# Shared weight pieces for two token streams at stage ends, four more modulation chunks on VectorE, and two holds in VectorE's queue

## Chip, cores and metric

One core of one Trainium2 chip runs the whole kernel in one launch. The metric is the device time of one execution in microseconds (us). The kernel before was run three times: median 2183.82 us, from 2181.91 to 2188.89.

## What is computed

The reference is two stacks of layers. The first has two layers on 256 tokens of 1024 channels (RMS norm, one wide projection, four kinds of mixing, output projection, residual) and a final norm. The second has two layers on two **streams**, the 256 latent tokens `x` (the first stack's output) and 256 context tokens `ctx`. Both go through the same weights, each with its own modulation:

```
for l in range(2):
    mod_l = silu(c) @ ada_w[l] + ada_b[l];  mod_c = silu(c_ctx) @ ada_w[l] + ada_b[l]   # 9 chunks of 1024 each
    xl = post_norm(xl, 0.5 * g1 * swiglu(modulate(xl, sh1, sc1), ffn1_w_in[l], ffn1_w_out[l]))   # "f1"; xc likewise
    yc, yl = even_mixer(...) if l == 0 else odd_mixer(...)       # gated linear attention + latent attention / windows
    xl = post_norm(xl, g2 * yl)
    xl = post_norm(xl, 0.5 * g3 * swiglu(modulate(xl, sh3, sc3), ffn2_w_in[l], ffn2_w_out[l]))   # "f2"
    # xc the same in layer 0; in layer 1 the context ends with f1 and its keys and values
```

`post_norm` adds the branch to `sqrt(2)` times the row and normalises it to mean 0 and variance 1; `modulate` scales and shifts by two chunks. The feed-forward width is 22 blocks of 128.

## The kernel before, in words

**Products in three parts.** Each fp32 product is made of three matmuls (`mm3`, L432 to 436): high by high, high by low, low by high. A weight **piece** of 128x1024 comes by a DMA of 512 KB on SyncE's queue (`wraw`, L394); ScalarE makes its high part `wh` (L353, called from `wload`), VectorE its low part `wl` by a subtraction (L428). There are four buffers each of the raw piece, `wh` and `wl`.

**Order.** The program is traced in Python order, and a planner then orders each engine's queue by its own estimate of when operands are ready, earlier traced first. Once built, the order in a queue is fixed, and an instruction that waits holds up all behind it. `issue_after(i)` makes what is traced under it stand behind `i` in the queue of `i`'s engine; it makes no other wait. `self.hold` is a list by which the next calls of `wload` put their ScalarE cast behind a given instruction.

**Modulation.** The 18 chunks (2 layers x 9) are vector by matrix products, made in one of two ways. `ada` (L600) does it on TensorE: 8 pieces per chunk, small matmuls (L620), for which it is a generator that `fill` advances between other steps. `ada_v` (L645) does it on VectorE: 8 steps per chunk, each one piece by DMA and two `scalar_tensor_tensor` with accumulation (L660), one per stream, advanced by `fillv`. Lists `V1`, `V2`, `V3` say which chunks VectorE makes during f1 of layer 0, f2 of layer 0 and f1 of layer 1: 5, 3 and 3. The other seven are TensorE's: (0,0), (0,1), (0,2) in the first stack, and (0,6), (0,7), (0,8), (1,1) later. `VR` has the steps per input tile and per output step.

**Feed-forward for two streams** (`ffn_two`, L866). Blocks of hidden columns go in groups of 8, 8 and 6. In the first group the first `F0` input tiles are done for ctx alone and then for x alone (so that x's norm has work beside it, 256 columns per matmul), the rest for both at once (512 columns). The last group's output products go stream by stream, ctx first: half n=0 of the 1024 output columns, then n=1, each with its own load of its 3 pieces (2 blocks each), so 12 loads; then the norm of that stream (`tail`, L769, interleaved with the last products, or `layernorm`, L581), and its modulation for the next stage (`xt_mod`, L542: 16 transposes on TensorE, L527, and for each of 8 blocks scale and shift, L558 or ScalarE, a cast to XTH on ScalarE and a subtraction to XTL, L560), put off by a few piece loads (`defer`). ctx's norm and modulation thus have x's products of both halves beside them.

**Mixer output** (`mixer_out`, L918) is the same in layer 0 with 4 pieces per half and stream: 16 loads. **Values of the odd mixer** (`odd_values`, L1761): per stream and half 4 pieces, 16 loads; x's modulation is flushed when its deferral runs out.

**Stage ends.** I number the five places where a norm and a modulation stand between stages: end 1 is f1 of layer 0 to the even mixer, end 2 the mixer output to f2, end 3 f2 to f1 of layer 1, end 4 f1 to the odd mixer, end 5 the odd mixer's output to f2 of layer 1 (x alone, `ffn_one`, L838).

Of the kernel before, what the change touches and what calls it, by code (L numbers as in the profile page):

```python
# [243 lines left out]
class Kern:  # L244
    def __init__(self, ctx, tc, A, out, stage=None):
# [29 lines left out]
        self.later, self.hold = [], []  # L275
# [129 lines left out]
    def wload(self, src, off, w, share=None):  # L405
        nc = self.nc
        if self.later:
            self.later[0][0] -= 1
            if self.later[0][0] < 0:
                with self.tc.issue_after(self.lastmm.ins):  # L410
                    self.later.pop(0)[1]()
        raw = self.wraw(src, off, w)
        h = self.wp.tile([P, 1024], F32R, tag="wh", name=f"wh{self.nm}", bufs=WB[1])
        hold = None
        if self.hold:
            hold = self.hold.pop(0)
# [12 lines left out]
        self.lastp = i  # L429
        return h, lo  # L430
# [287 lines left out]
    def ffn_in_steps(self, wi, ft, hid, ts, hs, pool, tag, share=None):  # L718

        nc = self.nc  # L720
        N = ts.stop - ts.start
        if N == 256:
            b = self.bank(tag)
            pgu = (b[:, :256], b[:, 256:])
        else:
            pgu = (self.bank(tag), self.bank(tag))
        for j in range(2):
            h, lo = self.wload(wi, (2 * ft + j) * 1024, 1024, share)
# [8 lines left out]
        self.split(hid[:, 0, hs], hid[:, 1, hs], pgu[1])  # L737
        yield
# [30 lines left out]
    def tail(self, rows, mul, gb, first, tag, done=None):  # L769
# [3 lines left out]
        for m, z in enumerate(rows):  # L773
# [3 lines left out]
            for i, (a, b) in enumerate(parts):  # L777
                o = self.bank(tag)
                mul(o[:, a:b], m, a, b)
                t = o[:, a:b]  # L780
# [15 lines left out]
            if m:  # L796
                h = slice(512, D)
                nc.vector.tensor_scalar(z[:, :512], z[:, :512], mv[:, 0:1], y, op0=OP.subtract, op1=OP.mult)
            self.act(z[:, h], z[:, h], AF.Identity, scale=y, bias=nb)
            if done:  # L800
                done(m)

# [63 lines left out]
    def ffn_two(self, name, l, pool, order, after, fills=(0, 0), vr=(0, 0), early={}):  # L866
# [8 lines left out]
        for f0 in range(0, NFT, G):  # L875
# [5 lines left out]
            if f0 == 0:  # L881
                for w in order:
# [3 lines left out]
                    for ft in range(0 if w == 0 else len(early), F0):  # L886
                        self.ffn_in(wi, ft, hid[ft], ts, ts, pool, "B", GX)
# [15 lines left out]
            else:  # L903
# [3 lines left out]
                for w in order:  # L907
                    for _ in self.ffn_out(wo, 0, f0, f1, hid, tiles(w), "A"):
                        pass
                    if TL[2 * (2 * l + int(name[1]) - 1) + w]:  # L910
                        self.ffn_tail(wo, f0, hid, tiles(w))
                    else:
                        for _ in self.ffn_out(wo, 1, f0, f1, hid, tiles(w), "A"):
                            pass
                        self.layernorm((self.X, self.C)[w])
                    self.defer(lambda w=w: after(w), DF[0] if w else DF[1])

    def mixer_out(self, src, l, who, pool):  # L918
        self.pnext = PN[4]
        gb = self.gate_rows(l, 1, who, pool)  # L920
        rows = (self.X, self.C)[who]
        outs = self.xs(src, 0, 512, 256 * who, 2)
        for m in range(2):
            self.accum(rows[m], 0, outs[m], gb, True)
        if TL[6 + who]:
            self.xs_tail(src, 4096, 256 * who, rows, gb)
        else:
            outs = self.xs(src, 4096, 512, 256 * who, 2, rows=ROWS)
            for m in range(2):
                self.accum(rows[m], 1, outs[m], gb, True)  # L930
            self.layernorm(rows)
# [40 lines left out]
    def layer1(self, l, b1):  # L972
# [13 lines left out]
        if l == 0:  # L986
# [774 lines left out]
    def odd_values(self, e, order):  # L1761
        V = [self.tl(e, [P, D], f"nv{m}") for m in range(4)]
        for w in order:
            for n in range(2):
                outs = self.xs(self.A["na"], 16 * 1024 + n * 4096, 512, 256 * w, 2)
                for m in range(2):
                    self.copy_any(V[2 * w + m][:, n * 512:(n + 1) * 512], outs[m])
# [50 lines left out]
    def run(self):  # L1818
# [47 lines left out]
        with tc.tile_pool(name="xd", bufs=1) as xc:  # L1866
# [3 lines left out]
            with tc.tile_pool(name="mo", bufs=1) as g:  # L1870
                self.gbn, self.accp = 1, g
                self.mixer_out(A["evo"], 0, 1, g)
                if stage > 5:
                    self.defer(lambda: self.xt_mod(0, 6, 1), DF[2])
                self.mixer_out(A["evo"], 0, 0, g)
                if stage > 5:
                    self.defer(lambda: self.xt_mod(0, 6, 0), DF[3])
# [110 lines left out]
```

## Time and profile before

| | |
|---|---|
| median of three runs | 2183.82 us |
| the profiled execution, its own time | 2177.1 us |
| its span, first to last instruction | 2175.3 us |
| around the span | 1.8 us |
| TensorE busy | 2097.1 us, 96% |
| VectorE, ScalarE busy | 1512.4 us, 70%; 868.0 us, 40% |
| mean granted TensorE clock | 0.986 |
| read from HBM | 332.94 MB |

The engines are named PE (TensorE), PEld (its weight loads), DVE (VectorE), ACT (ScalarE), POOL (GpSimd). PEclk is the granted TensorE clock: 1.00 is 2.4 GHz, 0.50 is 1.2 GHz. An engine's busy time says how much of a stretch it had an instruction running; in a stretch where TensorE is busy throughout, only less work on it shortens the time, and where it is idle, what it waited for does.

### The profile page before, as it was taken

What the parts mean: (1) busy time and instruction counts of PE and PEld (TensorE: products, weight loads), DVE (VectorE), ACT (ScalarE), POOL (GpSimd) and SP (SyncE); (2) the same over time, 40 slices, a digit from 0 to 9 for tenths busy, and PEclk for the clock granted to TensorE, in tenths of its full rate; (3) what the DMA queues carried; (4) which work ended last, traced back from release to release, by engine and by line L of the source; (5) the groups of instructions that cost most, each with busy time, mean ns of one, the idle gap of its engine ahead of it and who ended that gap; (6) DMA issues with size and microseconds to landing.
All of it is one profiled execution on the core that took longest, in us unless ns stands there. A gap on an engine that the chain in (4) does not pass through costs nothing.

```text
span 2175.3 us, 31944 instructions
## 1 busy us (share of the span) xinstructions
PE 2097.1 (96%) x12484; PEld 1769.3 (81%) x12484; DVE 1512.4 (70%) x2746; ACT 868.0 (40%) x1493; POOL 40.0 (2%) x78
## 2 busy tenths in 40 slices
PE   7999999999999899998999999899999989998998
PEld 5898798888877787887888888888888868887997
DVE  6977866667778775868466656846665676776666
ACT  5555545222223534544322223532222255654443
POOL 1000000000000000000000000000000010000000
PEclk9999999999999999999999999999999999998999
DMA  8545547656665312347444545544453364424663
GB/s 283 194 149 177 158 145 245 205 176 202 201 203 178 100 57 67 119 147 240 134 126 146 164 118 154 174 126 136 140 170 113 110 188 145 105 86 138 188 182 123
DMA packets 94903, 337.84 MB, mean 155 GB/s; under 512 B 11357, under 2 KB 12477, under 8 KB 94753
## 3 DMA queue, kind: packets, MB, share of 16 engines
q1 hardware_dynamic: 87552, 314.78, 46.8%
q0 software_dynamic: 5856, 17.39, 2.7%
q10 hardware_dynamic: 1344, 3.64, 0.5%
q8 instruction: 98, 1.61, 0.3%
q14 instruction: 53, 0.43, 0.1%
HBM read 332.94 MB, written 3.20 MB: 155 GB/s over the span
## 4 chain that ended last, share of the span: by engine, by line
PE 87%; DVE 7%; DMA 2%; ACT 2%; issue 2%; SPq 0%; ACTq 0%; DVEq 0%
PE pB L434 13%; PE pB L436 12%; PE pB L435 12%; PE pA L436 10%; PE pA L435 10%; PE pA L434 10%; PE pB L1483 2%; PE pF L434 2%; PE pF L436 2%; PE pF L435 2%; DVE wl L428 1%; PE pP L434 1%; PE pP L435 1%; PE pP L436 1%; DMA wr<-in_ada_dram 1%
## 5 line engine op out<-in xcount | busy, mean ns | idle before, releaser
L353 ACT ACTIVATE wh<-wr 128x1024 fp32r<-128x1024 f32 (+4 forms) x460 | 480.2, 1047 | 1022.5 <-issue 490.8
L428 DVE TENSOR_TENSOR wl<-wr,wh 128x1024 fp32r<-128x1024 f32 (+4 forms) x460 | 553.1, 1204 | 335.6 <-ACT wh L353 332.2
L434 PE MATMUL pB<-XTH,wh 128*128 128x512 f32 (+1 forms) x1552 | 539.3, 348 | 6.8 <-DVE hid L441 4.0
L436 PE MATMUL pB<-XTH,wl 128*128 128x512 f32 (+1 forms) x1552 | 535.3, 345 | 5.6 <-DVE wl L428 5.6
L435 PE MATMUL pB<-XTL,wh 128*128 128x512 f32 (+1 forms) x1552 | 535.6, 345 | 0.4 <-DVE XTL L560 0.4
L434 PEld LDWEIGHTS pB<-XTH,wh 128*128 128x128 f32 x1552 | 294.5, 190 | 48.5 <-DVE hid L441 4.4
L436 PEld LDWEIGHTS pB<-XTH,wl 128*128 128x128 f32 x1552 | 294.5, 190 | 43.9 <-DVE wl L428 5.8
L435 PEld LDWEIGHTS pB<-XTL,wh 128*128 128x128 f32 x1552 | 294.4, 190 | 38.2 <-DVE XTL L560 0.6
L435 PE MATMUL pA<-wl,hid 128*128 128x512 f32 (+1 forms) x624 | 239.5, 384 | 2.6 <-DVE wl L428 2.6
L436 PE MATMUL pA<-wh,hid 128*128 128x512 f32 (+1 forms) x624 | 239.5, 384 | 0.0
L434 PE MATMUL pA<-wh,hid 128*128 128x512 f32 (+1 forms) x624 | 238.0, 383 | 0.0
L660 DVE SCALAR_TENSOR_TENSOR vj<-wr,cb 128x1024 f32<-128x1024 f32 x176 | 214.9, 1221 | 11.7 <-DMA wr<-in_adav_dram 8.3
L736 DVE TENSOR_TENSOR pB<-ft,pB 128x512 f32<-128x512 f32 (+1 forms) x97 | 55.7, 574 | 136.2 <-PE pB L436 134.9
L435 PEld LDWEIGHTS pA<-wl,hid 128*128 128x128 f32 x624 | 117.2, 188 | 27.3 <-DVE wl L428 3.8
L434 PEld LDWEIGHTS pA<-wh,hid 128*128 128x128 f32 x624 | 117.1, 188 | 24.9 <-issue 0.6
L436 PEld LDWEIGHTS pA<-wh,hid 128*128 128x128 f32 x624 | 117.2, 188 | 22.8
L435 PE MATMUL pA<-wl,XTH 128*128 128x512 f32 (+4 forms) x336 | 125.0, 373 | 5.6 <-DVE wl L428 5.5
L434 PE MATMUL pA<-wh,XTH 128*128 128x512 f32 (+4 forms) x336 | 125.6, 376 | 0.4 <-ACT wh L353 0.4
L436 PE MATMUL pA<-wh,XTL 128*128 128x512 f32 (+4 forms) x336 | 125.5, 374 | 0.0
L575 DVE TENSOR_TENSOR pA<-pA,gb 128x512 f32<-128x512 f32 x84 | 58.0, 695 | 31.9 <-PE pA L436 31.7
L435 PEld LDWEIGHTS pA<-wl,XTH 128*128 128x128 f32 x336 | 64.7, 193 | 17.3 <-DVE wl L428 6.9
L434 PEld LDWEIGHTS pA<-wh,XTH 128*128 128x128 f32 x336 | 64.9, 193 | 12.3 <-ACT wh L353 0.7
(456 smaller groups left out, 2949.3 us busy)
## 6 DMA issues: line engine op xcount, KB each, us to landing
wr<-in_f1i_dram SPq DMA_DIRECT2D x108, 512.0 KB, 4.4
wr<-in_f2i_dram SPq DMA_DIRECT2D x94, 512.0 KB, 4.0
wr<-in_adav_dram SPq DMA_DIRECT2D x88, 512.0 KB, 3.9
wr<-in_ada_dram SPq DMA_DIRECT2D x56, 512.0 KB, 4.3
wr<-in_f1o_dram SPq DMA_DIRECT2D x56, 512.0 KB, 3.7
wr<-in_f2o_dram SPq DMA_DIRECT2D x50, 512.0 KB, 3.6
wr<-in_w_dram SPq DMA_DIRECT2D x40, 512.0 KB, 4.3
wr<-in_na_dram SPq DMA_DIRECT2D x32, 512.0 KB, 3.6
```

The source lines that it names most:

```text
L353: self.lasta = self.nc.scalar.activation(out, in_, func, **kw)
L428: i = eng.tensor_sub(lo[:, :w], raw[:, :w], h[:, :w].bitcast(F32))
L434: nc.tensor.matmul(out, lh, rh, start=start, stop=False)
L435: nc.tensor.matmul(out, lh, rl, start=False, stop=False)
L436: self.lastmm = nc.tensor.matmul(out, ll, rh, start=False, stop=stop)
L575: nc.vector.tensor_mul(p, p, gb[:, cs])
L660: nc.vector.scalar_tensor_tensor(junk, raw, 0.5 * f, cb[:, w], op0=OP.mult, op1=OP.mult, accum_out=gc[:, w, k:k + 1])
L736: nc.vector.tensor_mul(pgu[1], t, pgu[1])
L1483: nc.tensor.matmul(p[:, c0 + j * P:c0 + (j + 1) * P], K[r, j * 256 + tk * P:j * 256 + (tk + 1) * P], Q[r, j * 256 + tq * P:j * 256 + (tq + ...
```

## The change

VectorE gets 15 chunks in place of 11: V1 has 6, V2 has 4, V3 has 5; TensorE keeps the three of the first stack. A second list of holds, `holdl`, does for VectorE's subtraction of a piece what `hold` does for the cast: it is set to one entry after the last scaling of each first-stack layer's norm, and to four entries after the last tail's normalisation of end 5. `both_out` makes both streams' output products of a last group: one set of pieces for half n=0 of all four row tiles, one for n=1; after the first row tile of x's n=1 the modulation of ctx is put in (behind the last matmul so far). `mixer_out` and `ffn_two` use it. `ffn_two` keeps the pieces of ctx's last `F0` tile and does that tile first for x. `odd_values` goes ctx n=0, ctx n=1, x n=1 with the same pieces, x n=0.

```diff
-V1 = ((0, 3), (0, 4), (0, 5), (1, 0), (1, 2))
-V2 = ((1, 3), (1, 4), (1, 5))
-V3 = ((1, 6), (1, 7), (1, 8))
-VR = ((2.0, 0.5), (1.25, 0.25), (1.25, 0.25))
+V1 = ((0, 3), (0, 4), (0, 5), (0, 6), (0, 7), (0, 8))
+V2 = ((1, 0), (1, 1), (1, 2), (1, 3))
+V3 = ((1, 4), (1, 5), (1, 6), (1, 7), (1, 8))
+VR = ((2.4, 0.5), (1.75, 0.25), (2.2, 0.25))
...
-        i = eng.tensor_sub(lo[:, :w], raw[:, :w], h[:, :w].bitcast(F32))
+        hold = self.holdl.pop(0) if self.holdl else None
+        with self.tc.issue_after(hold.ins) if hold else ExitStack():
+            i = eng.tensor_sub(lo[:, :w], raw[:, :w], h[:, :w].bitcast(F32))
...
+    def both_out(self, pieces, mul, streams, first, ends, tag, after):
+        ws = pieces(0)
+        alls = streams[0][1] + streams[1][1]
+        self.row_products(ws, lambda o, i, a, b: mul(ws, o, alls[i], a, b), alls, 0, first, tag)
+        w1 = pieces(1)
+        for i, (rows, tiles) in enumerate(streams):
+            def hook():
+                if i == 1:
+                    with self.tc.issue_after(self.lastmm.ins):
+                        after(0)
...
+            if ends[i]:
+                self.tail(rows, m1, tiles[0][1], first, tag, hook=hook)
+            else:
+                self.row_products(w1, m1, tiles, 1, first, tag, hook)
+                self.layernorm(rows)
+        after(1)
...
+                    fs = list(range(0 if w == 0 else len(early), F0))
+                    if keep:
+                        fs = fs[-1:] + fs[:-1]
+                    for ft in fs:
+                        self.ffn_in(wi, ft, hid[ft], ts, ts, pool, "B", GX, keep if ft == F0 - 1 else None)
...
+        self.holdl = [scaled]
         self.fill(FB1[0][l])
         self.xt_scaled(xn, self.cols[:, C_NW + 8 * l:C_NW + 8 * l + 8], 0)
...
-                self.gbn, self.accp = 1, g
-                self.mixer_out(A["evo"], 0, 1, g)
...
+                self.gbn, self.accp = 2, g
+                self.mixer_out(A["evo"], 0, g, lambda i: self.defer(lambda: self.xt_mod(0, 6, 0), DF[3]) if i
+                               else self.xt_mod(0, 6, 1))
...
                     self.xt_mod(1, 6, 0)
+                    self.holdl = [self.lastn] * 4
```

## Rows read from the trace of the kernel before

**Rows 1.** Page, part 1: busy us, share of the span, instructions.

```profile
PE 2097.1 (96%) x12484; PEld 1769.3 (81%) x12484; DVE 1512.4 (70%) x2746; ACT 868.0 (40%) x1493; POOL 40.0 (2%) x78
```

**Rows 2.** Busy time by stretch, stage ends 1 to 5: length, busy, PEclk, DMA, GB/s.

```profile
684.00:725.00 41.00, 33.72 (x199) 28.55 (x200) 35.75 (x92) 14.02 (x25) 3.31 (x7) 0.92 0.57 185
1011.00:1028.00 17.00, 11.54 (x84) 10.13 (x84) 13.58 (x27) 10.49 (x21) 0.00 (x0) 1.00 0.88 324
1377.50:1390.00 12.50, 6.94 (x39) 6.73 (x37) 11.49 (x30) 4.04 (x7) 0.54 (x1) 0.73 0.50 158
1758.00:1789.00 31.00, 22.02 (x89) 17.43 (x88) 21.37 (x51) 14.83 (x25) 5.54 (x9) 0.83 0.76 220
1961.00:1994.00 33.00, 22.37 (x144) 20.97 (x144) 20.21 (x42) 14.64 (x26) 0.56 (x1) 0.79 0.48 144
```

**Rows 3.** Busy time by stretch, L620 alone: length, PE, PEld, PEclk, DMA.

```profile
350.00:700.00 350.00, 11.18 (x320) 8.26 (x320) 1.00 0.63 202
700.00:1000.00 300.00, 8.76 (x192) 5.40 (x192) 0.95 0.33 105
```

**Rows 4.** Page, part 5, groups of L428 and L660: busy, mean ns, idle before.

```profile
L428 DVE TENSOR_TENSOR wl<-wr,wh 128x1024 fp32r<-128x1024 f32 (+4 forms) x460 | 553.1, 1204 | 335.6 <-ACT wh L353 332.2
L660 DVE SCALAR_TENSOR_TENSOR vj<-wr,cb 128x1024 f32<-128x1024 f32 x176 | 214.9, 1221 | 11.7 <-DMA wr<-in_adav_dram 8.3
```

**Rows 5.** Busy time by stretch, f1 of layer 0: last input tiles, last output products.

```profile
595.00:667.00 72.00, 72.00 (x365) 57.33 (x363) 52.20 (x75) 19.48 (x26) 0.00 (x0) 1.00 0.60 192
668.00:690.00 22.00, 20.71 (x93) 16.34 (x89) 21.95 (x36) 7.27 (x9) 2.23 (x4) 1.00 0.49 152
```

**Rows 6.** Busy time by stretch, even mixer, around its second fall of the clock.

```profile
867.20:877.50 10.30, 10.04 (x50) 7.72 (x48) 6.93 (x11) 1.07 (x2) 1.14 (x2) 0.50 0.23 67
```

**Rows 7.** Timeline, DVE, start of the kernel: start, us, instruction, idle before.

```profile
8.70 0.21 DVE L373 TENSOR_SCALAR nwt<-nwt 128x1 f32<-128x1 f32 x1
11.19 1.20 DVE L428 TENSOR_TENSOR wl<-wr,wh 128x1000 fp32r<-128x1000 f32 x1 [2.28 <-ACT wh L353]
...
13.30 0.75 DVE L984 TENSOR_SCALAR xn<-X,nwy 128x1024 f32<-128x1024 f32 x1
```

**Rows 8.** Timeline, DVE, the second layer's norm.

```profile
170.03 1.22 DVE L428 TENSOR_TENSOR wl<-wr,wh 128x1024 fp32r<-128x1024 f32 x1
```

**Rows 9.** Groups of instructions, PE, 172.3 to 178.2 us: busy, mean ns, idle before.

```profile
L436 PE MATMUL pG<-XTH,wl 128*128 128x256 f32 x16 | 4.6, 285 | 0.0
```

**Rows 10.** Timeline, DVE, end 1: first and last of the context's chain.

```profile
686.39 1.29 DVE L575 TENSOR_TENSOR pA<-pA,gb 128x512 f32<-128x512 f32 x2
...
710.31 0.76 DVE L560 TENSOR_TENSOR XTL<-pF,XTH 128x256 fp32r<-128x256 f32 x2
```

**Rows 11.** Timeline, DVE, end 3: the context's chain and the piece behind it.

```profile
1360.56 0.69 DVE L575 TENSOR_TENSOR pA<-pA,gb 128x512 f32<-128x512 f32 x1
...
1380.80 0.42 DVE L560 TENSOR_TENSOR XTL<-pF,XTH 128x256 fp32r<-128x256 f32 x1
...
1382.75 1.17 DVE L428 TENSOR_TENSOR wl<-wr,wh 128x1024 fp32r<-128x1024 f32 x1
```

**Rows 12.** Timeline, PE, two matmuls of 512 columns one after the other.

```profile
1359.04 0.39 PE L435 MATMUL pA<-wl,hid 128*128 128x512 f32 x1
1359.27 0.39 PE L436 MATMUL pA<-wh,hid 128*128 128x512 f32 x1
```

**Rows 13.** Waits, ACT, first from 1003 to 1019 us, then from 1765 to 1780 us: total, times, longest.

```profile
ACT wh L353 <- DMA wr<-in_f2i_dram: 8.5, 4, 4.8
...
ACT wh L353 <- DMA wr<-in_na_dram: 9.2, 3, 6.7
```

**Rows 14.** Timeline, DVE, end 5: first and last subtraction ahead of the norm.

```profile
1962.45 1.22 DVE L428 TENSOR_TENSOR wl<-wr,wh 128x1024 fp32r<-128x1024 f32 x1
...
1965.38 1.20 DVE L428 TENSOR_TENSOR wl<-wr,wh 128x1024 fp32r<-128x1024 f32 x1
...
1968.78 0.54 DVE L798 TENSOR_SCALAR X<-X,lnmv,nwy 128x512 f32<-128x512 f32 x1
```

More of the change, by code (lines that the diff above doesn't have):

```diff
@@ L274, in __init__ @@
         self.ptn = 3
-        self.later, self.hold = [], []
+        self.later, self.hold, self.holdl = [], [], []
         self.vfrac = 0.0
@@ L727, in ffn_in_steps @@
         for j in range(2):
-            h, lo = self.wload(wi, (2 * ft + j) * 1024, 1024, share)
+            if ws and len(ws) == 2:
+                h, lo = ws[j]
+            else:
+                h, lo = self.wload(wi, (2 * ft + j) * 1024, 1024, share)
+                if ws is not None:
+                    new.append((h, lo))
             self.ws(pgu[j], h, lo, ts)
@@ L767, in ffn_out, with tail @@
             self.accum(z, n, o, gb, f0 == 0)
-    def tail(self, rows, mul, gb, first, tag, done=None):
+    def tail(self, rows, mul, gb, first, tag, done=None, hook=None):
         nc = self.nc
@@ L779, in tail @@
                 mul(o[:, a:b], m, a, b)
+                if hook and m == 0:
+                    hook()
                 t = o[:, a:b]
@@ L801, in tail, with row_products, m1 @@
                 done(m)
+    def row_products(self, ws, mul, tiles, n, first, tag, hook=None):
+        for i, (z, gb, _) in enumerate(tiles):
+            o = self.bank(tag)
+            mul(o, i, 0, 512)
+            if hook and i == 0:
+                hook()
+            self.accum(z, n, o, gb, first)
+    def both_out(self, pieces, mul, streams, first, ends, tag, after):
[8 more added lines that the diff above has]
+                        after(0)
+            def m1(o, m, a, b):
+                mul(w1, o, tiles[m], a, b)
+            if ends[i]:
+                self.tail(rows, m1, tiles[0][1], first, tag, hook=hook)
+            else:
+                self.row_products(w1, m1, tiles, 1, first, tag, hook)
+                self.layernorm(rows)
+        after(1)
     def ffn_tail(self, wo, f0, hid, tiles, done=None):
@@ L906, in ffn_two @@
                 self.fillv(1000)
[L907 to L916, printed above, removed]
@@ L918, in mixer_out @@
-    def mixer_out(self, src, l, who, pool):
-        self.pnext = PN[4]
[L920 to L931, printed above, removed]
+                us = range(f0, NFT, 2)
@@ new lines, in mul @@
+                def mul(ws, o, t, a, b):
+                    for u, w in zip(us, ws):
+                        for j in range(2):
+                            hh, s = hid[u + j - f0], slice(t[2], t[2] + P)
+                            js = slice(j * 512 + a, j * 512 + b)
+                            self.mm3(o, hh[:, 0, s], hh[:, 1, s], w[0][:, js], w[1][:, js], u + j == f0, u + j == NFT - 1)
+                k = 2 * (2 * l + int(name[1]) - 1)
+                self.both_out(lambda n: [self.wload(wo, (n * NFT + u) * 512, 1024) for u in us], mul,
+                              [((self.X, self.C)[w], tiles(w)) for w in order], False, [TL[k + w] for w in order], "A",
+                              lambda i: self.defer(lambda: after(order[1]), DF[1]) if i else after(order[0]))
@@ new lines, in mixer_out, with mul @@
+    def mixer_out(self, src, l, pool, after):
+        self.pnext = PN[4]
+        streams = []
+        for w in (1, 0):
+            gb = self.gate_rows(l, 1, w, pool)
+            rows = (self.X, self.C)[w]
+            streams.append((rows, [(rows[m], gb, 256 * w + m * P) for m in range(2)]))
+        def mul(ws, o, t, a, b):
+            s = slice(t[2], t[2] + P)
+            for k in range(8):
+                w, js = ws[k // 2], slice(k % 2 * 512 + a, k % 2 * 512 + b)
+                self.mm3(o, self.XTH[:, k, s], self.XTL[:, k, s], w[0][:, js], w[1][:, js], k == 0, k == 7)
+        self.both_out(lambda n: [self.wload(src, n * 4096 + 1024 * u, 1024) for u in range(4)], mul, streams, True,
+                      (TL[7], TL[6]), "A", after)
@@ L1762, in odd_values, with put @@
         V = [self.tl(e, [P, D], f"nv{m}") for m in range(4)]
-        for w in order:
-            for n in range(2):
-                outs = self.xs(self.A["na"], 16 * 1024 + n * 4096, 512, 256 * w, 2)
-                for m in range(2):
-                    self.copy_any(V[2 * w + m][:, n * 512:(n + 1) * 512], outs[m])
+        src, o = self.A["na"], 16 * 1024
+        a, b = order
+        def put(w, n, outs):
+            for m in range(2):
+                self.copy_any(V[2 * w + m][:, n * 512:(n + 1) * 512], outs[m])
+        put(a, 0, self.xs(src, o, 512, 256 * a, 2))
+        ws = []
+        for w in (a, b):
+            outs = [self.pA(), self.pA()]
+            for u in range(4):
+                if w == a:
+                    ws.append(self.wload(src, o + 4096 + u * 1024, 1024))
+                elif u == 0:
+                    self.flush()
+                for m in range(2):
+                    s = slice(256 * w + m * P, 256 * w + (m + 1) * P)
+                    for j in range(2):
+                        js = slice(j * 512, (j + 1) * 512)
+                        self.mm3(outs[m], self.XTH[:, 2 * u + j, s], self.XTL[:, 2 * u + j, s], ws[u][0][:, js], ws[u][1][:, js],
+                                 u + j == 0, u == 3 and j == 1)
+            put(w, 1, outs)
+        put(b, 0, self.xs(src, o, 512, 256 * b, 2))
         return V
```

17 lines of the change are left out of this document (8 added, 9 removed).

## The prediction

> **What bounds it now.** I read the page's busy shares first: TensorE is busy for 96% of the span, VectorE for 70% [rows 1]. So two things shorten the time: work taken off TensorE where it never idles, and the waits that hold it up. Next I looked where TensorE idles, by busy time in stretches, and found most of it at the stage ends [rows 2]: length less busy is 7.3, 5.5, 5.6, 9.0 and 10.6 us at ends 1 to 5, 38 of the 78 us that are idle in all. The reader should see PEclk there too. It is 0.92, 1.00, 0.73, 0.83 and 0.79, and as the clock has two levels, the share at 1.2 GHz is twice what is missing: 6.6, 0, 6.8, 10.5 and 13.9 us, in which up to half is lost wherever TensorE works. Then the queue of VectorE: it is busy 21.95 of 22 us before end 1 [rows 5] and 11.5 of 12.5 at end 3 [rows 2]. A piece's subtraction for the next stage stood at 1382.75 behind the rest of the context's and latents' norms [rows 11], and TensorE stood for it. A stage end is a VectorE problem.
>
> **Part 1: four chunks from TensorE to VectorE.** In f1 of layer 0 TensorE spends 11.2 us on L620 [rows 3] at full business (72.00 of 72.00 us in a sample of it [rows 5]). That goes, and with it some 2 us of transposes and one wait on those loads; call it 13. In the even mixer L620 holds 8.8 us [rows 3]. There the work is a chain of short products with gaps that the chunks fill, so the gain lies between 0 and 8.8; I take 4. VectorE gains 4 chunks of 16 operations at 1221 ns [rows 4]: 78 us. It loses subtractions of shared pieces: 8 in the mixer output, 18 in three feed-forward ends, 6 by the kept tile, 4 in the values, 36 at 1204 ns [rows 4], 43 us; ScalarE loses as many casts, SyncE's queue as many of 512 KB. Does VectorE have room? Input tiles of f1 are the densest: 52.2 of 72 us [rows 5], a little over six tiles; 0.4 steps more per tile are 2.4 steps of 2.44 us, giving 58 of 72, 81%. TensorE had no idle time at 73%, and 1.3 us in 22 at full VectorE [rows 5]. The cost thus lies between 0 and that share of 15 such tiles' 180 us, 11 us; 81% is nearer the first, so 0. By the rates in VR the first feed-forward makes 2.4x15 + 0.5x16 = 44 of 48 steps on its way, before it was 38 of 40, so two more steps plus the last tile's 0.4, some 6 us of VectorE, fall into end 1. Two transfers swap queues with nothing: both kinds are 512 KB on SyncE's.
>
> **Part 2: pieces for both streams.** TensorE's products are the same. At a feed-forward end six subtractions go, 7.2 us, at the mixer output eight, 9.6 us, out of stretches where VectorE is full. In exchange the context's chain (last sum, norm, 16 transposes, modulation) loses cover. Before, all of x's products stood beside it; now only x's n=1: two row tiles of 18 matmuls at 0.23 us [rows 12], 8.3 us, plus 1.6 for the transposes, at the mixer 11 plus 1.6. The chain took 20.7 us at end 3 and 24.7 at end 1 [rows 10, 11], but of that it needs some 10 us of VectorE by itself; the rest was other streams' work and seven or so subtractions, two to four of which stay. I expect the chain at 12 to 13 us and a wait of 2 to 3 where 5.6 stood.
> - End 1: 7.2 us of subtractions go, 6 us of steps come. Nearly nothing changes: -1.
> - End 2: ScalarE's casts waited 8.5 us for loads [rows 13] while DMA moved 324 GB/s [rows 2]. With the last pieces held since ctx's n=1, the four raw buffers are free for f2's pieces some 11 us sooner: -2 of 5.5.
> - End 3: of 5.6 idle and up to 3.4 of half clock, -4.
> - End 4: of 9.0 and up to 5.2, -5. A part of it is loads again, 9.2 us of waits of the casts [rows 13], which delay a normalisation behind them in ScalarE's queue; earlier raw buffers help, the mixer's bias loads stay.
>
> The bounds of the four together: all of it back, 27.4 idle plus 11.9 of clock, and on the other side the rivals below. The tile first done for x from kept pieces, and the values from kept pieces, lie beside a TensorE that is busy; 0. The values hold all four buffers for x's n=1, so the next four casts follow one by one over 11 us; they need 2.3 each: 0.
>
> **Part 3: the holds.** At the start VectorE's next instruction after L373 at 8.7 was a subtraction that waited 2.28 us for its cast and ran 1.20 [rows 7]; the norm's last scaling stood behind it to 13.30. Behind it instead it costs nothing, as its cast is ready by then: -3.4 at most, -3 taken. At end 5 three subtractions, 1962.45 to 1966.58 [rows 14], and one before stand in the last tile's norm; the norm's queue loses 3.6 us. Queued behind it they wait for nobody, but the four must then share VectorE with the modulation that TensorE waits for, which has gaps. Between 0 and 10.6 plus half of 13.9; I take -4, the 3.6 and a bit of clock. In the second layer the norm ends with the queue full; but there the first piece loaded after the hold is set is not the layer's own. `fill` comes first, and it loads a piece of ctx's early feed-forward tile. The subtraction at 170.03 [rows 8] moves behind the norm, and the 48 matmuls that fill TensorE during it (the row has a third of them [rows 9]) get a third of one half late. If TensorE can run the other 40 first, the price is 1 us against 0.6 gained; if not, 48 of some 0.12 us, 5.9. I take +0.5.
>
> **The sum.** -13 -4 -1 -2 -4 -5 -3 -4 +0.5 = -35.5. The profiled execution took 2177.1 us, 2175.3 of span and 1.8 around it; it becomes 2141.6. It lies 6.7 below the median, so against the median 2148.3; I say **2148**.
>
> **Two rules weighed.** At end 2 the wait stands beside 324 GB/s [rows 2]. The Trainium skill, "DMA: Bandwidth & Descriptors", Specifications, gives about 358 GB/s as what a core gets from HBM; by it that wait is bandwidth and stays, and the sum would be 2 us less of a gain. For the even mixer, the trace shows a 10.3 us stretch at PEclk 0.50 though TensorE was busy 10.04 of it [rows 6]. The Trainium skill, "TensorE: Matmul & The Clock Gate", What's actually happening, says the slow clock is the resting state and activity lifts it. It speaks against taking filler from TensorE; by it the rival "clock" below gains weight.
>
> **The rivals.**
> - **The ends only move** (0.15). The shorter cover eats what the subtractions give: ends 1 to 4 gain nothing, 12 us less: 2160. For: VectorE stays full at end 1. Against: 26 subtractions, 31 us of VectorE, leave these ends and 6 us come.
> - **Slower: the context's chain in the open** (0.09). If the planner lets x's sums, held pieces and leftover steps go ahead of it, the chain stays as long as today at its worst or longer, say 27 us from the context's last product to its last XTL block, with TensorE at 9.9 us of cover (12.6 at end 2): three waits of 17 and one of 14, 66 us, and 3 us of half clock each, 78, where idle time and clock cost up to 39 today. That is +39 against -23.5 from the rest: 2199. It turns slower from some 23 us per chain on. For: 24.7 at end 1 today [rows 10]. Against: the 10 us it needs.
> - **The clock and VectorE take the chunks back** (0.08). In the even mixer the gaps open, one more fall like the one of 10.3 us [rows 6] costs 5 in place of -4, and VectorE's backlog costs the 11: 9 + 11 = +20, 2168.
> - **The hold does another thing** (0.06): in the second layer it holds the filler and not the layer, 5.4 more: 2154.
> - **All waits at the ends go** (0.08): 39 in place of 12: 2121.
>
> The forecast has 0.54. A measurement of this kernel can tell about 0.3%, 6.6 us, from no change. Slower by that is the second rival, 0.09. The third together with the first comes to 2180, 0.05 for the same. The rest, 0.86, is faster. The range takes in the forecast with its bounds, the first, third and fourth rival: 2128 to 2172; outside are the slower rival, most of the last and a twentieth of tails, under 0.2.
>
> **What would show it.** L620 has 384 instructions in place of 896 and none after 350 us; L660 240 in place of 176, L428 some 424. TensorE stays full between 400 and 650 us, and f1 of layer 0 is 13 us shorter. At the start the second scaling comes near 10 us. At end 3 the wait on L428 is under 3 us and PEclk nearer 1. At end 5 no L428 stands between the last sum and L798. The prediction is wrong if ends 1 to 4 idle as long as today, if TensorE waits for L428 within the input tiles, or if the even mixer takes as long as before.

## The result, and the profile after

The changed kernel takes 2156.97 us (median of four runs, 2155.68 to 2157.61), the kernel before in the same comparison 2182.86: the ratio is 0.9876, 95% interval 0.9856 to 0.9897. It is 25.9 us faster; I had said 2148, with a range from 2128 to 2172. The profiled execution took 2157.57 us with a span of 2155.8, so it stands at its own median, while that of before stood 6 to 7 us below its median. Two spans compared therefore show 19.5 us.

Page, part 1, of the changed kernel, to be held against [rows 1]:

```profile
PE 2082.2 (97%) x11967; PEld 1760.7 (82%) x11967; DVE 1549.3 (72%) x2834; ACT 829.5 (38%) x1450; POOL 36.8 (2%) x73
```

TensorE is busy 14.9 us less, and idle 73.6 us in place of 78.2. So three quarters of the span's gain is less busy time, one quarter is less waiting. The small matmuls that left had held 20 us [rows 3]; against that, the time at half clock rose from 62 to 73 us (mean granted clock 0.986 and 0.983), of which up to half is lost. Busy time by stretch, ends 1 to 5 of the changed kernel (columns as in [rows 2]):

```profile
674.00:721.00 47.00, 39.40 (x214) 32.75 (x212) 41.47 (x104) 12.57 (x22) 3.29 (x7) 0.85 0.39 134
1000.00:1017.50 17.50, 12.82 (x96) 12.38 (x95) 10.34 (x23) 6.81 (x16) 0.00 (x0) 0.90 0.74 278
1365.00:1378.00 13.00, 11.18 (x71) 9.04 (x69) 13.00 (x35) 7.83 (x15) 0.53 (x1) 1.00 0.44 131
1745.00:1776.00 31.00, 24.00 (x102) 18.63 (x101) 20.22 (x51) 14.97 (x26) 5.47 (x9) 0.89 0.71 204
1945.00:1975.00 30.00, 23.04 (x150) 21.12 (x149) 20.62 (x44) 15.48 (x27) 0.56 (x1) 0.83 0.51 159
```

Length less busy is now 7.6, 4.7, 1.8, 7.0 and 7.0 us, 28.1 in place of 38.0. End 3 is nearly closed, ends 1 and 2 idle nearly as long as they did, ends 4 and 5 lie between. PEclk shows more: end 1 has 13.7 us at half clock where before had 6.8, and end 2 has 3.4 where before had none. As the ends gave back 9.9 us of idle time but the whole kernel only 4.6, some 5 us of new idle time stand elsewhere. To find them I took the times of a few landmarks from TensorE's timeline, first or last instruction of a kind, in us from the span's start:

| landmark on TensorE | before | after | shift |
|---|---|---|---|
| first output product of the first layer | 150.36 | 153.27 | +2.9 |
| last transpose of the second layer's normed rows | 183.02 | 189.53 | +6.5 |
| first output product of the second layer | 314.45 | 324.03 | +9.6 |
| first key by query product of the even mixer | 764.55 | 761.28 | -3.3 |
| last product of its latent attention | 956.00 | 946.01 | -10.0 |
| first output product of f2, layer 0 | 1098.76 | 1089.61 | -9.2 |
| last output product of f1, layer 1 | 1758.27 | 1745.13 | -13.1 |
| first product with the odd mixer's values | 1836.20 | 1820.89 | -15.3 |
| last product of its output | 1961.56 | 1945.91 | -15.7 |
| first output product of the last f2 | 2025.40 | 2006.21 | -19.2 |
| end of the span | 2175.32 | 2155.79 | -19.5 |

Most stretches came within 3 us of the forecast. The large miss stands at the start: the first stack, where I had summed -2.5, is 9.6 us **longer**. Its two holds are the change there. Timeline of VectorE in the second layer's norm, changed kernel:

```profile
173.81 0.75 DVE L1041 TENSOR_SCALAR xn<-X,nwy 128x1024 f32<-128x1024 f32 x1
...
179.55 0.75 DVE L1041 TENSOR_SCALAR xn<-X,nwy 128x1024 f32<-128x1024 f32 x1
180.22 2.35 DVE L430 TENSOR_TENSOR wl<-wr,wh 128x1024 fp32r<-128x1024 f32 x2
```

and TensorE's timeline beside it:

```profile
180.36 1.33 PE L529 MATMUL pB<-ident,xn 128*128 128x128 f32 x5 [4.37 <-DVE xn L1041]
181.49 0.58 PE L438 MATMUL pG<-XTH,wl 128*128 128x256 f32 x1
```

No subtraction stands between the two scalings, where one of the filler's (the early feed-forward tile of ctx) had stood at 170.03 [rows 8]. TensorE waits 4.37 us for the second scaling, and the filler's `pG` products that had covered it [rows 9] come behind the transposes. At the other hold, at the start, the scaling came 3.3 us sooner (10.01 against 13.30 [rows 7]), but TensorE then waited for something else (waits of PE, 10 to 25 us):

```profile
PE pG L622 <- DMA wr<-in_ada_dram: 3.3, 2, 1.7
PE pB L529 <- DVE xn L1041: 0.9, 1, 0.9
```

### The profile page after: what moved, and what is told of

Its sections match the earlier page's. It is cut to its first block, busy times and chain, and to the rows that moved or that the text cites. A ratio compares the mean times of both kernels' runs of the same rounds, so it can differ in the third digit from the quotient of the medians.

```text
span 2155.8 us, 30795 instructions
## 1 busy us (share of the span) xinstructions
PE 2082.2 (97%) x11967; PEld 1760.7 (82%) x11967; DVE 1549.3 (72%) x2834; ACT 829.5 (38%) x1450; POOL 36.8 (2%) x73
## 4 chain that ended last, share of the span: by engine, by line
PE 87%; DVE 6%; DMA 2%; ACT 2%; issue 2%; SPq 0%; ACTq 0%; DVEq 0%
PE pB L436 13%; PE pB L437 13%; PE pB L438 13%; PE pA L436 10%; PE pA L438 10%; PE pA L437 10%; PE pF L436 2%; PE pF L438 2%; PE pF L437 2%; PE pB L1541 1%; DMA wr<-in_ada_dram 1%; PE pP L436 1%; PE pP L437 1%; PE pP L438 1%; ACT wh L353 1%
## 5 line engine op out<-in xcount | busy, mean ns | idle before, releaser
L353 ACT ACTIVATE wh<-wr 128x1024 fp32r<-128x1024 f32 (+4 forms) x424 | 442.2, 1045 | 1010.5 <-issue 458.6
L430 DVE TENSOR_TENSOR wl<-wr,wh 128x1024 fp32r<-128x1024 f32 (+4 forms) x424 | 509.3, 1203 | 303.5 <-ACT wh L353 299.9
L662 DVE SCALAR_TENSOR_TENSOR vj<-wr,cb 128x1024 f32<-128x1024 f32 x240 | 293.0, 1221 | 4.0
```

The lines of the kernel that those rows point to most:

```text
L353: self.lasta = self.nc.scalar.activation(out, in_, func, **kw)
L662: nc.vector.scalar_tensor_tensor(junk, raw, 0.5 * f, cb[:, w], op0=OP.mult, op1=OP.mult, accum_out=gc[:, w, k:k + 1])
```

## Experiments

All times are medians with their ratio to the kernel before, run beside them on the same chip. Kernels of different comparisons ran on different chips, where the median of before lay between 2179.8 and 2182.9, so a few us between two of them count only if the ratios or the landmarks show them too. "Landmark" means a place like those in the table above, in the same profiled execution.

### The two holds of the first stack

Taken out together:

```diff
-        self.holdl = [scaled]
         self.fill(FB1[0][l])
```

> The changed kernel with the hold behind the norm's last scaling taken out in both layers of the first stack; the hold at end 5 stays. Theory (the two holds cost what the first stack lost): the first output product of f1 in layer 0, 7.6 us later than before in the changed kernel, comes within 1 us of the kernel before or up to 2 earlier, and the time is 2157.0 - 9.6 = 2147.4 us, from 2145 to 2150. Rival (the first stack loses for another reason, such as the planner's order for the shorter list of chunks): that product stays 6 us or more late and the time is between 2155 and 2159.

2150.98 us, 0.9863 (0.9844 to 0.9882): 6 us less than the changed kernel's median and 3 less by the ratios, whose intervals overlap. The landmark missed: the first output product of f1 stood at 415.41, 4.5 us later than before's 410.92, where I had expected it within 1 us or up to 2 earlier. So the holds were part of it only. Keeping the first one:

```diff
-        self.holdl = [scaled]
+        if l == 0:
+            self.holdl = [scaled]
```

> The changed kernel with the hold in the first layer of the first stack only. Theory (the changed kernel's landmarks read as a sum: +2.9 by the first layer's output, +6.7 in the second): 2157.0 - 6.7 = 2150.3 us, slower than without both holds by 2.9. Rival (the start hold gains its 3 us as predicted, and the 2.9 come from the chunks on TensorE waiting for their loads in both cases): 2144 to 2146, faster than without both holds.

2152.82 us, 0.9865 (0.9845 to 0.9885): slower than either expectation, and not to be told from no hold.

What filled the gap were the other kernels below. Nine of the profiled executions, that of before among them, have the same first 2490 TensorE products in the same order, which before makes up to 330 us. In them the second layer's first output product stands at 314.45 (before), 316.07, 316.18, 317.17, 318.09, 318.45, 320.36, 320.87 and 321.10: a mean of 318.1 and a spread of 6.7 us with nothing changed. They differ in waits for chunk pieces and in falls of the clock to 1.2 GHz; the wait of 2.68 us that ended at 227.13 in before, without a fall, had a fall within 2 us of its end in all eight others (in one of them the wait was 2.22 us). **Before's profiled execution was the earliest of the nine**, 3.6 us ahead of the mean. Against the mean the changed kernel is late by 5.9. Counted from the first layer's output, its last transpose of the second layer's rows is 3.6 late (36.3 us against 32.7).

To settle which hold costs this I put each back alone into a faster kernel (all_three, below). The two ran in one comparison, all_three itself in another.

```diff
+        if l:
+            self.holdl = [scaled]
         self.fill(FB1[0][l])
```

> all_three with the changed kernel's hold in the second layer of the first stack only, before the filler's call. Theory (this hold is most of what the first stack lost: it holds the filler's subtraction, the 48 matmuls that cover the norm come behind it): TensorE waits 4 us or more for the second layer's scaled rows, the last transpose of those rows stands 3.5 us later to the first layer's output than in all_three, the time is 2127.2 + 4 to 6, 2131 to 2133. Rival (the first stack's loss was the spread of its clock and loads, which differ by 6 us between runs of one and the same order of matmuls): the time is within 1.5 us of 2127.

2132.08 us, 0.9779 (0.9765 to 0.9792), 4.9 above all_three, 3 by the ratios, and 5.1 above the kernel with the other hold, which ran beside it. Waits of PE, 170 to 192 us, first of this kernel:

```profile
PE pB L529 <- DVE xn L1043: 4.4, 1, 4.4
```

then of all_three:

```profile
PE pB L529 <- DVE xn L1043: 0.3, 1, 0.3
```

The second layer's first output product stood at 323.39, 5.3 later than the mean, and the last transpose came 3.4 us later than in all_three, counted from the first layer's output. Counted from the first layer's first output product, the second scaling itself came 1.4 us sooner with the hold (26.3 us against 27.7): the norm gained, and TensorE lost its cover.

```diff
+        if l == 0:
+            self.holdl = [scaled]
         self.fill(FB1[0][l])
```

> all_three with the changed kernel's hold in the first layer of the first stack only. Theory (the norm's last scaling comes 3 us sooner, but then TensorE waits as long for the chunk pieces, which land at 18 to 21 us whatever VectorE does, and falls to half clock once more): the first transposes end 3 us earlier, the first layer's output at the same time within 1.5 us, 2126 to 2129. Rival (the prediction's term: the 3 us stay): 2123 to 2125.

2126.95 us, 0.9754 (0.9740 to 0.9767), the same as all_three's 2127.19. The first transposes ended 3.2 us sooner (16.80 against 20.01), and the first layer's output came at 153.64, later than in all nine executions above. Waits of PE, 10 to 25 us, of this kernel:

```profile
PE pG L622 <- DMA wr<-in_ada_dram: 2.2, 2, 1.8
PE pB L529 <- DVE xn L1043: 0.9, 1, 0.9
```

and of all_three:

```profile
PE pB L529 <- DVE xn L1043: 3.9, 1, 3.9
...
PE pA L437 <- DVE wl L430: 0.5, 1, 0.5
```

The two chunk pieces that TensorE needs next landed at 18.52 and 20.95 us with the hold, at 19.70 and 20.95 without. The start is bound by the first loads; the prediction's 3 us do not stay. Last, the second layer's hold set one line later, so that it falls on the layer's own piece:

```diff
         self.fill(FB1[0][l])
+        if l:
+            self.holdl = [scaled]
```

> The same as all_three, and in the second layer of the first stack alone a hold that is set behind the call that loads the filler's piece, so that it holds the layer's own first piece and not the filler's. Theory (the hold of the changed kernel cost its 4 us because it held the filler's subtraction, and 48 matmuls that cover the norm came late): the last transpose of the second layer's rows stays within 0.7 us of all_three relative to the first layer's output, and the time within 1.5 us of all_three. Rival (any hold in that place opens the wait on the norm, as the filler is ordered anew): that transpose comes 3 us or more later and the time is 3 to 5 us above all_three.

2125.99 us, 0.9766 (0.9738 to 0.9794): the same as without. The transposes end 0.5 us sooner after the first layer's output, and the wait on the scaled rows is gone from the list. The second scaling comes 26.3 us after the first layer's output, as early as with the bad hold. So it is not a hold in that place that costs the time, but which subtraction it caught.

### The parts alone

The new lists and rates of chunks on the kernel before (`V1`, `V2`, `V3`, `VR`, as in the diff of the change, nothing else):

> The kernel before with the new lists of chunks and their rates alone: no shared pieces, no holds. Theory (chunks leave a full TensorE, and VectorE still has room within the input tiles): f1 of layer 0 with its end 11 to 13 us shorter, the even mixer 6 to 7 shorter, the ends at most 4 longer: 2182.9 - 18 = 2165 us, from 2160 to 2168. Rival (the room for the chunks comes from the 36 subtractions that the shared pieces save, 43 us of VectorE): TensorE waits for subtractions in f1 of layer 1 and at the ends, and the time is 2171 or more.

2174.22 us, 0.9966 (0.9952 to 0.9981): 7.6 faster, the rival's side, though f1 of layer 1 did not lose. Busy time by stretch in f1 of layer 0 (as [rows 5]):

```profile
595.00:667.00 72.00, 72.00 (x313) 58.44 (x311) 61.93 (x91) 22.01 (x27) 0.00 (x0) 1.00 0.60 193
668.00:690.00 22.00, 11.32 (x36) 7.64 (x35) 22.00 (x42) 3.45 (x4) 0.50 (x1) 0.74 0.28 89
```

Within the tiles TensorE is full although VectorE is 86% busy, but at the end VectorE works 22.00 of 22.00 us and TensorE 11.32. From f1's first output product to its last, TensorE idled for 10.7 us and ran 13.7 at half clock (up to 6.8 lost) where before had 2.6 and none: nearly all of what the chunks gave in that stretch. Its largest wait from 660 to 705 us is for VectorE's sums of the context's rows:

```profile
PE pA L434 <- DVE C L579: 5.6, 3, 2.7
```

In the changed kernel these stretches, 10 us earlier, read

```profile
585.00:657.00 72.00, 72.00 (x311) 58.12 (x310) 56.91 (x81) 19.01 (x24) 0.00 (x0) 1.00 0.57 169
658.00:680.00 22.00, 22.00 (x97) 17.93 (x97) 20.31 (x34) 5.04 (x6) 0.00 (x0) 1.00 0.53 158
```

The other half: the old lists and rates, no holds, shared pieces alone (the changed kernel less three edits).

> The changed kernel with the old lists of chunks and rates and without any of the holds: pieces for both streams alone. Theory (the rest of the sum: ends 1 to 4 give some 10 us, the values among them): 2182.9 - 10 = 2173 us, from 2169 to 2176. Rival (the ends only move, the context's chain losing as much cover as the subtractions give): 2180 to 2184. If this and the chunks alone add up to the time without layer holds less 3.5 of end 5's hold, the parts are independent.

2159.49 us, 0.9892 (0.9869 to 0.9916): 22 faster, better than either expectation. Its profiled execution was the slowest of the four (2164.15), 13.2 us of span under that of before. By the landmarks from f1's first output product on, end 1 gave 8.2, end 3 4.4 and end 4 with the values 3.9, end 2 took 1.4. At end 1 no wait on VectorE of any size is left (waits of PE, 700 to 724 us):

```profile
PE pA L436 <- ACT XTH L353: 1.7, 3, 0.9
PE pF L529 <- DVE XTL L562: 0.2, 1, 0.2
```

Both parts with end 5's hold come to 30.8 (no_layer_holds), and without any hold to 27.3 (no_end5_hold, next section), where the two alone sum to 29.9. So the parts add up within the noise, and the test in that expectation is met. The profiled executions from the second layer's first output product to the end say 8.2 us for the chunks alone and 11.7 for the chunks on top of the pieces. Of that, 2.8 and 4.5 come before the even mixer's first key by query product, that is in f1 with end 1, and 6.1 and 6.8 in the even mixer. So the chunks lose most of f1's gain with the pieces too, only in another place: TensorE then stays full to f1's last output product, but from there to the last X transpose it takes 27.4 us, where the pieces alone take 17.3. That it is the steps left over which cost this is tested below (earlier_steps).

### End 5's hold

```diff
                     self.xt_mod(1, 6, 0)
-                    self.holdl = [self.lastn] * 4
```

on top of no_layer_holds.

> The changed kernel without any of the holds. Beside 2151.0 us without the first stack's holds. Theory (the hold at end 5 is worth what its landmark showed, 2.7 us by the last X transpose and 3.5 by the first output product of the last f2): 2154 to 2155, and no time moves before 1940 us. Rival (the four subtractions cost the same behind the norm as inside it, and the 3.5 us came from the clock): 2150 to 2152.

2153.31 us, 0.9870 (0.9854 to 0.9886), 2.3 more, which the medians alone don't prove. The stretch does: from the odd mixer's last output product to the last f2's first takes 64.2 us here, 63.8 before, 62.7 and 64.0 in the two kernels of the section above, all without the hold; in the ten kernels with it 60.3 to 61.6, mean 60.8. The mean difference is 2.8 us. Waits of PE, 1930 to 1975 us, without the hold:

```profile
PE pF L529 <- DVE X L811: 4.2, 1, 4.2
PE pF L529 <- ACT X L353: 3.1, 1, 3.1
```

and in the changed kernel, 1938 to 1975 us:

```profile
PE pF L529 <- DVE X L811: 2.6, 1, 2.6
PE pF L529 <- ACT X L353: 1.2, 1, 1.2
```

### What still stands at ends 1, 2 and 4

Three edits, each on no_layer_holds (2151.0). First, the chunk steps that the rates leave over for end 1 are moved into the tiles:

```diff
-VR = ((2.4, 0.5), (1.75, 0.25), (2.2, 0.25))
+VR = ((2.7, 0.5), (1.75, 0.25), (2.2, 0.25))
```

> The changed kernel without the two holds of the first stack, and 2.7 in place of 2.4 chunk steps per input tile of f1 in layer 0. Beside the same without this edit, 2151.0 us. Theory (VectorE has room within the input tiles, 81% full by the prediction; the steps left over for end 1, 14 operations of 1.22 us between 673 and 688, keep the context's norm waiting): f1 of layer 0 stays within 1 us, end 1 (27.7 us from the last product before it to the last X transpose) gets 4 to 7 us shorter, the time 2144 to 2147. Rival (VectorE is at its limit within the tiles): TensorE waits for subtractions or chunk steps before 680 us, and the time is 2151 or more.

(The 14 operations start between 663 and 686 us, eight of them after 673.) 2142.56 us, 0.9825 (0.9806 to 0.9844). The stretch from f1's last output product to the last X transpose is 19.1 us in place of 27.7, and TensorE stays full before it at 82% of VectorE:

```profile
582.00:654.00 72.00, 72.00 (x312) 58.46 (x312) 58.94 (x87) 18.74 (x24) 0.00 (x0) 1.00 0.56 177
655.00:677.00 22.00, 22.00 (x98) 17.92 (x97) 20.19 (x32) 4.35 (x6) 0.50 (x1) 1.00 0.22 68
...
671.00:712.50 41.50, 38.46 (x234) 33.21 (x233) 34.88 (x93) 14.49 (x27) 3.30 (x7) 0.96 0.37 129
```

Waits of PE at that end on no_layer_holds, 692 to 722 us:

```profile
PE pF L529 <- DVE C L594: 3.8, 2, 2.7
PE pA L438 <- DVE wl L430: 2.5, 1, 2.5
```

and with the edit, 688 to 714 us, where the context's norm is gone from the list and six operations in place of 14 are left behind the first product of the last group:

```profile
PE pA L436 <- ACT XTH L353: 2.6, 3, 1.3
```

Second, end 4. The odd mixer's first bias loads go behind the pieces of its first products:

```diff
-                        nc.gpsimd.dma_start(b[64 * rl:64 * rl + 64],
+                        with self.tc.issue_after(self.lastd.ins) if h2 < 4 else ExitStack():
+                            (nc.sync if h2 < 4 else nc.gpsimd).dma_start(b[64 * rl:64 * rl + 64],
```

(`lastd` is the latest piece load.)

> The changed kernel without the two holds of the first stack, and the first eight loads of the odd mixer's biases (4 MB in 128 half tiles' worth of rows, issued from 1746 to 1751 us ahead of the first value piece) put on the queue of the pieces behind the pieces of the mixer's first products. Beside 2151.0 us. Theory (end 4's wait of 6.0 to 6.4 us for x's normalisation is a load: ScalarE's cast waits for a piece behind those biases, and the normalisation stands behind the cast): the value piece lands 5 us or more earlier, the wait at the first X transpose falls under 2 us and its fall of the clock goes, 2144 to 2147. Rival (the casts are not what the normalisation waits for, or the pieces are late anyway): the wait stays over 4 us and the time within 1 us of 2151.

(The eight loads are 256 KB each, 2 MB; the 4 MB of that text is a slip.) 2147.28 us, 0.9838 (0.9818 to 0.9858); from f1's last output product to the last X transpose 21.1 us in place of 29.3. Waits of ScalarE, 1744 to 1764 us, of the changed kernel:

```profile
ACT wh L353 <- DMA wr<-in_na_dram: 10.4, 2, 10.1
```

and the loads issued from 1744 to 1758 us:

```profile
nb<-in_bias_dram POOLq DMA_DIRECT2D x8, 256.0 KB, 5.9
wr<-in_na_dram SPq DMA_DIRECT2D x4, 512.0 KB, 10.3
```

With the edit, the loads of the same stretch, and TensorE's waits from 1740 to 1766 us, where a wait of 6.4 us for x's normalisation on ScalarE had stood:

```profile
wr<-in_na_dram SPq DMA_DIRECT2D x6, 512.0 KB, 4.8
```

```profile
PE pA L436 <- ACT wh L353: 0.7, 1, 0.7
PE pF L529 <- DVE X L811: 0.6, 1, 0.6
```

So the normalisation was late because it is queued on ScalarE behind a cast, the cast because its piece was in transfer among 2 MB of biases, which the changed kernel first uses at 1815.6. Third, the same at end 2, where four chunk pieces and two broadcasts were issued ahead of f2's third input piece:

```diff
-                nc.gpsimd.dma_start(cb[:, w], ...)
+                with self.tc.issue_after(self.lastd.ins) if items is V2 else ExitStack():
+                    (nc.sync if items is V2 else nc.gpsimd).dma_start(cb[:, w], ...)
...
+                with self.tc.issue_after(self.lastd.ins) if (l, c) == V2[0] and k < 4 else ExitStack():
                     raw = self.wraw(A["adav"][l], (c * KD + k) * D, D, self.ring)
```

> The changed kernel without the two holds of the first stack, and the first four chunk pieces of f2 in layer 0 and the two broadcasts of the condition rows (3 MB, issued at 990 us ahead of the third input piece of f2) put behind the input pieces beside which their steps are traced. Beside 2151.0 us. Theory (end 2's wait of 4.5 us with half of 3.4 is that third piece's load, 494 KB short of nothing else): the piece lands 4 us or more earlier, the wait falls under 1 us, 2146 to 2148. Rival (DMA is full there whatever the order, as the gate rows and later pieces take its place, or TensorE waits for something else of f2's first tile): the wait stays over 3 us, 2150 to 2152.

2145.00 us, 0.9831 (0.9815 to 0.9848). Loads issued from 987 to 1000 us in the changed kernel:

```profile
wr<-in_f2i_dram SPq DMA_DIRECT2D x5, 512.0 KB, 10.3
wr<-in_adav_dram SPq DMA_DIRECT2D x4, 512.0 KB, 10.3
cb<-srow POOLq DMA_DIRECT2D x2, 512.0 KB, 10.1
gb<-g POOLq DMA_DIRECT2D x2, 512.0 KB, 14.6
```

and from 984 to 997 us with the edit, with the busy time of end 2 (second line of the ends above):

```profile
wr<-in_f2i_dram SPq DMA_DIRECT2D x5, 512.0 KB, 4.5
gb<-g POOLq DMA_DIRECT2D x2, 512.0 KB, 6.1
```

```profile
994.00:1011.50 17.50, 17.42 (x147) 17.21 (x146) 14.78 (x38) 10.32 (x22) 0.00 (x0) 1.00 0.50 169
```

TensorE has no wait left there, and the stretch from the last product of latent attention to the last X transpose takes 63.2 us in place of 69.7. All three together:

> The changed kernel without the two holds of the first stack, with 2.7 chunk steps per input tile, with the bias loads behind the odd mixer's first pieces and with the chunk loads of f2 behind its input pieces. Theory (each edit takes one stage end's wait: 9.0 us by the last X transpose of end 1, 7.0 at end 2, 8.2 at end 4, read in the separate kernels against the one without holds; they lie some hundreds of us apart and so add): 2151.0 less the three medians' gains (8.4, 6.0, 3.7 us) is 2133, less the three landmarks' gains 2127: from 2125 to 2134, and faster than both kernels. Rival (what one edit saves is lost later, as the waits only move on): 2139 or more.

2127.19 us (2125.86 to 2133.10), 0.9765 (0.9741 to 0.9789): 53 us under the kernel before; under the changed kernel it is by 30 in the medians and by 24 in the ratios, so it is **faster than both**; the intervals of the two ratios lie apart. The three ends stay closed side by side, 18.8, 63.2 and 20.3 us in the stretches that took 27.7, 69.7 and 29.3. Something else came with them: the even mixer, from its first key by query product to the last product of latent attention, takes 180.2 us with 6.8 at half clock, where no_layer_holds takes 184.7 with 17.1. The three kernels built on all_three take 180.1 to 180.9, the three with one edit each 184.2 to 185.6, and no run shows which edits together do it. Page, part 1:

```profile
PE 2068.8 (97%) x11967; PEld 1750.4 (82%) x11967; DVE 1549.5 (73%) x2834; ACT 829.8 (39%) x1450; POOL 31.1 (1%) x63
```

## Why the prediction was right, and where it failed

| step | predicted | by the landmarks |
|---|---|---|
| holds in the first stack | -3 +0.5 | +9.6 |
| f1 of layer 0 with end 1 | -13 -1 | -12.9 |
| even mixer | -4 | -6.7 |
| end 2 | -2 | +0.8 |
| end 3 (to the last output product of f1) | -4 | -4.0 |
| end 4 with the values | -5 | -2.2 |
| odd mixer, hold of end 5 | -4 | -3.9 |
| last f2 | 0 | -0.3 |
| sum | -35.5 | -19.5 |

**The step that failed is the hold in the second layer.** I had seen that it catches the filler's subtraction, and took +0.5, the case in which TensorE runs the other 40 matmuls first, over 5.9. It doesn't: in the changed kernel all but two of the 48 come behind the first transposes of the late scaling, TensorE waits 4.4 us, and the runs give 3.4 us by the last transpose and about 5 in the times, the far end of the bound. The rival that named this was the true case, at 0.06. The **start hold's -3** failed as well: it is 0, since I looked for the wait that ends and not for what is late next, the first chunk pieces. With 5.9 and 0 for these two the sum against the median is 2156.7, and 2157.0 was measured. That it comes so close is in part luck: the even mixer gave 2.7 us more than its term, ends 2 and 4 together 5.6 less. The other 3.6 us of the 9.6 are the early execution that I summed against.

**The chunks** moved as worked out: L622 is left with 384 instructions, the last at 273.7 us, L662 has 240 and L430 424, all as named. These groups of the changed kernel, as [rows 4]:

```profile
L430 DVE TENSOR_TENSOR wl<-wr,wh 128x1024 fp32r<-128x1024 f32 (+4 forms) x424 | 509.3, 1203 | 303.5 <-ACT wh L353 299.9
...
L662 DVE SCALAR_TENSOR_TENSOR vj<-wr,cb 128x1024 f32<-128x1024 f32 x240 | 293.0, 1221 | 4.0
```

Their cost of 0 in the input tiles held, at 79% of VectorE (I had 81%), but the reason was incomplete. chunks_only and earlier_steps show that room within the tiles isn't enough: what is left over for the end must have room there too, and neither the old pieces nor the shared ones give it. That f1 with end 1 came to -12.9 against -14 is a balance of three terms. Beside the pieces, the chunks made the way to f1's last output product 14.7 us shorter (13 forecast) and the stretch behind it 10.1 longer (6 us of steps forecast; both no_end5_hold against shared_pieces_only). The pieces alone gave 8.6, or 8.2 from f1's first output product on (7.2 forecast). Moving eight of the 14 left-over operations out gave 8.6 back. So each term has the right sign, the cost of the steps was sized too small, and the three misses nearly cancel.

**The even mixer** gave 6.7 of 8.8, nearer the whole than the half I took. Its time at half clock fell from 20.5 to 17.1 us in all, so the rival by which the clock takes the chunks back did not come. The Trainium skill, "TensorE: Matmul & The Clock Gate", What's actually happening, on the resting state of the clock spoke for that rival; no run here shows it for these chunks.

**Ends 2 and 4** were mis-sized for one reason: "earlier raw buffers help". The casts' waits on loads were 8.5 and 9.2 us [rows 13] and are now 8.2 and 10.4, since the buffer was not what the piece waited for. Other loads were in front. At end 2 the prediction had weighed that the wait is bandwidth and stays, 2 us less of a gain, and in the changed kernel it did stay. The Trainium skill, "DMA: Bandwidth & Descriptors", Specifications, gives about 358 GB/s as a core's limit from HBM; the kernel before moved 417 GB/s from 350 to 360 us, so here the measurement decides. And chunk_loads_behind closes that end at 169 GB/s, with the same loads in the whole kernel: in the changed kernel the DMA engines were busy there (0.74 of the stretch, 0.50 with the edit) with pieces that nobody needed yet, and the wait was the order of the loads. End 4's gain came from the values instead (46.6 us from the last X transpose to the first product with them, 49.2 before), which I had costed at 0.

**End 3** (4.0 of 4) and **end 5** (2.8 by the means, 3.5 in the changed kernel, of 4) were near their size, and the signs named for them came: at end 3 no wait on L430 is left and PEclk is 1.00; at end 5 no L430 stands between the last sum (1946.41) and L811 (1949.61). The slower rival, the context's chain in the open, is refuted by the waits: the largest at ends 1 to 3 are 2.7, 4.5 and 0.9 us, and the 4.5 is a load. "The ends only move" is refuted by shared_pieces_only.

What stays open: from the last X transpose before it to its last key by query product the even mixer still idles for 8.8 us and runs 17.1 at half clock (up to 8.5 lost) in the changed kernel. No run here set out to change that, and why all_three has less half clock there is not shown. The falls of the clock within the first stack I can count, not predict.

## What to carry to other kernels

Before you hold an instruction behind another, list which instruction the hold will catch and what the engine next in line would have run meanwhile; a norm that ends 1.4 us sooner cost 3 to 5 us here, as its cover came late. When work moves to an engine with room on average, look for room at the stage's end, where what is left over lands in front of the norm. When a cast waits for its load, read what was issued in the 10 us before on every queue: moving 2 and 3 MB of early loads behind such a piece gained 8 and 6.5 us here, by the landmarks.

## What the runs showed of the hardware that I had not expected

A 512 KB piece issued into quiet queues landed after 3.4 us (f2's first, issued at 987.16, landed at 990.53); issued some us behind chunk pieces on its own queue and beside broadcasts on GpSimd's, it took 10.3. The Trainium skill, "DMA: Bandwidth & Descriptors", Queues, rings and completion order, says that each DMA engine goes round between the queues that have work; the end 4 rows agree, where the piece is first of its kind on SyncE's queue and still took 9.7 us beside GpSimd's eight. From 1750 to 1758 us the DMA engines are busy throughout and move 227 GB/s, where in the kernel before they move 417 from 350 to 360 us; why they are slower there is not shown.

One and the same order of 2490 products spread by 6.7 us over the first 320 us, and the clock fell to 1.2 GHz within 2 us of the same wait in eight of the nine executions and not in the ninth. A sum against one profiled execution carries that spread; the landmarks of several are needed before a term of a few us in such a stretch can be called measured.
